# A gated HGRN2 and pooling block: the pool products spread over two gate steps, operand sums one per step, RMS roots computed on GpSimd

## The chip, the cores and the metric

The kernel runs on one core of a Trainium2 chip. The metric is the device time of one execution in microseconds (us); the number that counts is the median over several runs. The engines are named as in the profile: PE is TensorE (PEld its weight loads), DVE is VectorE, ACT is ScalarE, POOL is GpSimd, and SP is SyncE, which in this kernel computes nothing and issues most of the DMAs, in its own order.

## The reference

One decoder block over 1024 tokens of width 1024, all in float32:

```
proj = x @ w_in -> [q | f | i | og | pool_v | gate_a | gate_b]        # 7 x 1024 columns
f = lb + (1 - lb) * sigmoid(f_pre);  k = 1 - f
S_t = diag(f_t) S_{t-1} + k_t v_t^T;  o_t = S_t^T q_t                  # 8 heads of 128, chunks of 16
o = o * rsqrt(mean(o^2) + 1e-6) * hgrn_norm_g * sigmoid(og)            # per head
a = o @ w_a
b = (causal_mean_w(pool_v) - pool_v) @ w_pool[g] * pool_scale          # 4 groups of 256, windows 2, 4, 8, 16
mix = (sigmoid(gate_a) * a + sigmoid(gate_b) * b) @ w_out
x = LN(2^0.25 * x + mix);  x = LN(2^0.25 * x + relu(x @ w_up)^2 @ w_down)
```

## The kernel before

Every large product is done in float32 precision by three products of a high and a low part: an operand is copied on ACT into its high part (line 125) and the rest is taken on DVE into its low part (line 126), so each operand costs one ACT copy and one DVE subtraction. On top of that, a product of two by two blocks is done in seven block products instead of eight, with sums of blocks as operands. The function `pair` writes out these seven steps for one pair of 128 output columns: each step is an operand (`t0`, `b_21`, `t2`, `t3`, `t1`, `t4`, `b_22`) and a product of twelve matmuls of 512 columns (`p1` to `p3`, all through `prod`, lines 206 to 214). The sums of weight blocks are made on DVE in place, in the raw blocks: `make_t3` makes one, and `make_t2` makes two at once (lines 287 to 291). The results of the seven products are put together by copies out of PSUM on ACT (line 274) and sums on DVE (line 278); the `takes` then apply the sigmoid and store the result to a scratch tensor in DRAM.

The middle of the kernel is the recurrence over eight heads and two halves of the tokens. It is a generator, `recurrence`, that hands out small pieces of work. `run` calls it once after every product of twelve matmuls ("a turn"), so the recurrence's small matmuls stand between the large ones. A half takes 8.5 turns (`PER_HALF`). In its first turn come the outputs of the half before (`outputs`), the transposed keys and the scores; in the turn `TURN_BACK` = 4 the outputs are transposed (`turn_outputs`, line 990), multiplied by gain and gate (line 992) and sent off (`put_output`, lines 629 to 637), and the states of the half are made. The other turns prepare the next half, chiefly on DVE, with some small operations on POOL (lines 863 to 882). `outputs` squares the four chunks on ACT with a running sum (line 980), takes the root on ACT (line 981), the reciprocal on DVE (line 982), and scales on ACT (line 984). Sigmoid and root are functions of different ACT tables, so both come with an ACT_TABLE_LOAD.

`ORDER` (line 33) gives the columns that are done beside the recurrence: the inputs of the heads, the pool values (`pooled`), the output gates, and the gates 0 to 6. The order on PE is written out by hand in this part (`manual_schedule`, line 1035); the other engines and SP are ordered by a scheduler that works by a timeline of its own, and the order is then fixed. After the recurrence, lines 1043 to 1048 do `pool_products(0)` to `pool_products(3)` and then `gates(7)`. One `pool_products(g)` loads w_pool[g] and four tiles of pooled values, splits them into high and low parts, and makes four products of six matmuls each into PSUM tiles "pj" (lines 732 to 752). Each is multiplied on DVE by the scale and by a gate that is loaded back (line 751), and stored. The tiles for the loads ("raw", a ring of six) and for the parts of pooled values ("w", a ring of ten) are those of the weight blocks; q, f, v and og of the recurrence hold the gates and results. After that come the product with w_a, in pairs, then w_out with the first norm, then w_up and w_down.

All tiles are rings of a few buffers: a new tile of a ring waits until an older one has been read for the last time, by engines or by DMAs.

Of the kernel before, what the change touches and what calls it, by code (L numbers as in the profile page):

```python
# [11 lines left out]
U32 = mybir.dt.uint32  # L12
AF = mybir.ActivationFunctionType
ALU = mybir.AluOpType
# [16 lines left out]
TURN_BACK = 4  # L31
# [4 lines left out]
    ("gates", 2), ("inputs", 7), ("pooled", 3), ("gates", 3), ("gates", 4), ("gates", 5), ("gates", 6),  # L36
)
PRIO_WHOLE = 6000
# [12 lines left out]
def tile_hybrid_block(  # L51
# [191 lines left out]

    def w_part(src):
        return split(src, w_tile)
# [20 lines left out]
    def pair(raw, rooms, takes, pz_tag="pj", twin=False, pc_tag="pj", turned=False):  # L266
# [18 lines left out]
        def make_t2():  # L285
            if turned:
                V.tensor_sub(b12, b11, b12)
                minus_sum(b11, b22, b12)
            else:
                V.tensor_sub(b12, b12, b11)  # L290
                V.tensor_sub(b11, b22, b12)

# [10 lines left out]

        def t4():
# [8 lines left out]
        def t1():  # L313
            return w_part(b12)
# [106 lines left out]
    with tc.tile_pool(name="xr", bufs=8, side="right", reuse_waits="tile") as xr:  # L421
# [34 lines left out]
        def load_x(u, w):  # L456
            rows_of = x2[u * HALF : (u + 1) * HALF, w].rearrange("(t p) c -> p t c", p=P)
            nc.sync.dma_start(out=x_rows[u][:, :, w], in_=rows_of)
# [30 lines left out]
        load_x(1, slice(HALF, D))  # L489
# [152 lines left out]
    with tc.tile_pool(name="tmp", bufs=1, side="right", reuse_waits="tile") as tmp:  # L642
# [25 lines left out]
        def head_inputs(h, behind=()):  # L668
# [13 lines left out]
            def take_q(u):  # L682
# [5 lines left out]

            run(pair(
                loaded_blocks(w_in, h * P, D + h * P), (c_soon, c_late, room_f),  # L690
# [21 lines left out]
        def gates(j):  # L712
            spare = j == KT - 1
            rooms = [lambda tag=tag: tt(tag) for tag in ("q", "f", "og")] if spare else (c_soon, c_late, c_late)

            def take(dst, src=None, more=None):
                def put(t):
                    s = (tt("v") if spare else c_late()) if src else t
                    more_of = loaded(more, lambda: tt("v")) if more is not None else None
                    A.activation(s, t, AF.Sigmoid)  # L720
                    if more_of is not None:
                        V.tensor_mul(s, s, more_of)
                    nc.sync.dma_start(out=dst if more is None else more, in_=s)
                return put

            more = pbd[j] if spare else (None, None)
            run(pair(
                loaded_blocks(w_in, 5 * D + j * P, 6 * D + j * P), rooms,
                (take(gad[j][0]), take(gbd[j][0], True, more[0]), take(gad[j][1]), take(gbd[j][1], False, more[1])),
            ))  # L730

        def pool_products(g):

            rooms = iter(("v", "q", "f", "og"))
# [300 lines left out]
        with tc.manual_schedule(engines={mybir.EngineType.PE}):  # L1035
# [7 lines left out]
            for _ in turns:  # L1043
                pass
# [441 lines left out]
```

## Time and profile before

| | us |
|---|---|
| median of 3 runs | 1473.27 (1473.22 to 1474.59) |
| the profiled execution | 1472.62 |
| its span in the trace | 1470.8 |
| PE busy in it | 1438.0 |
| DVE busy | 1100.2 |
| ACT busy | 760.8 |
| POOL busy | 107.4 |

The span runs from the first to the last instruction of the program; 1.8 us of the execution's time lie around it. A busy PE is not a PE at full rate: a matmul's end is modelled, so short waits and a lowered clock are seen better in the number of matmuls that fit into a stretch. In the stretches without a wait and with nothing but matmuls of 512 columns, 134 of them fit into 30 us.

The stages by time from the start of the span: the values (up to about 97 us), the recurrence with the columns beside it (to about 606 us), the pool products (about 619 to 650 us), the last gate and w_a, w_out and the first norm (to about 850 us), w_up, and w_down to the end.

### The profile page before, as it was taken

What the parts mean: (1) busy time and instruction counts of PE and PEld (TensorE: products, weight loads), DVE (VectorE), ACT (ScalarE), POOL (GpSimd) and SP (SyncE); (2) the same over time, 40 slices, a digit from 0 to 9 for tenths busy, and PEclk for the clock granted to TensorE, in tenths of its full rate; (3) what the DMA queues carried; (4) which work ended last, traced back from release to release, by engine and by line L of the source; (5) the groups of instructions that cost most, each with busy time, mean ns of one, the idle gap of its engine ahead of it and who ended that gap; (6) DMA issues with size and microseconds to landing.
All of it is one profiled execution on the core that took longest, in us unless ns stands there. A gap on an engine that the chain in (4) does not pass through costs nothing.

```text
span 1470.8 us, 20899 instructions
## 1 busy us (share of the span) xinstructions
PE 1438.0 (98%) x7377; PEld 1189.8 (81%) x7377; DVE 1100.2 (75%) x1807; ACT 760.8 (52%) x1383; POOL 107.4 (7%) x288
## 2 busy tenths in 40 slices
PE   8999999999999999979999999999999999999997
PEld 7788888788878888858788878888888888888886
DVE  4967876896897796467985598566666787777977
ACT  5545566665755655545542366555556543333435
POOL 0002111211211210000002100000000100000000
PEclk9999999999999999989999999999999999999999
DMA  7142245345435536797663134444447874435422
GB/s 258 58 136 87 76 127 165 79 137 152 107 93 145 136 87 174 247 337 256 223 230 114 58 100 174 137 154 156 144 151 264 275 263 150 163 131 170 129 72 115
DMA packets 187738, 229.21 MB, mean 156 GB/s; under 512 B 12240, under 2 KB 110576, under 8 KB 187632
## 3 DMA queue, kind: packets, MB, share of 16 engines
q1 hardware_dynamic: 181664, 213.96, 43.9%
q0 software_dynamic: 5184, 11.54, 4.0%
q10 hardware_dynamic: 784, 2.38, 0.5%
q8 instruction: 58, 0.95, 0.3%
q14 instruction: 48, 0.39, 0.1%
HBM read 150.22 MB, written 77.59 MB: 155 GB/s over the span
## 4 chain that ended last, share of the span: by engine, by line
PE 88%; DVE 5%; DMA 4%; issue 1%; ACT 1%; SPq 0%; POOL 0%; DVEq 0%; ACTq 0%
PE ps_pj L211 15%; PE ps_pj L214 15%; PE ps_pj L213 15%; PE ps_pj L1369 4%; PE ps_pj L1367 4%; PE ps_pj L1368 4%; PE ps_pj L112 2%; PE ps_pj L113 2%; PE ps_pj L114 2%; PE ps_tr L1369 1%; PE ps_tr L1367 1%; PE ps_tr L1368 1%; PE ps_sc L211 1%; PE ps_sc L213 1%; PE ps_sc L214 1%
## 5 line engine op out<-in xcount | busy, mean ns | idle before, releaser
L211 PE MATMUL ps_pj<-act,w 128*128 128x512 f32 x1068 | 420.5, 394 | 8.3 <-ACT c L274 2.9
L214 PE MATMUL ps_pj<-act,w 128*128 128x512 f32 x1068 | 416.0, 391 | 2.3 <-DVE w L126 2.3
L213 PE MATMUL ps_pj<-act,w 128*128 128x512 f32 x1068 | 415.3, 390 | 0.0
L125 ACT CAST w<-raw 128x512 fp32r<-128x512 f32 x326 | 202.3, 622 | 289.8 <-PE ps_pj L213 200.9
L126 DVE TENSOR_TENSOR w<-raw,w 128x512 fp32r<-128x512 f32 x326 | 222.8, 686 | 107.2 <-ACT w L125 101.0
L211 PEld LDWEIGHTS ps_pj<-act,w 128*128 128x128 f32 x1068 | 200.9, 188 | 53.6 <-ACT c L274 4.5
L214 PEld LDWEIGHTS ps_pj<-act,w 128*128 128x128 f32 x1068 | 200.8, 188 | 46.4 <-DVE w L126 3.9
L213 PEld LDWEIGHTS ps_pj<-act,w 128*128 128x128 f32 x1068 | 201.0, 188 | 40.5
L1329 ACT CAST act<-act 128x1024 fp32r<-128x1024 f32 x66 | 67.1, 1050 | 109.0 <-issue 35.0
L278 DVE TENSOR_TENSOR c<-c,ps_pj 128x512 f32<-128x512 f32 x95 | 64.7, 682 | 43.5 <-PE ps_pj L214 41.5
L1368 PE MATMUL ps_pj<-act,act 128*128 128x512 f32 x240 | 93.0, 389 | 0.0
L1369 PE MATMUL ps_pj<-act,act 128*128 128x512 f32 x240 | 93.0, 389 | 0.0
L1330 DVE TENSOR_TENSOR act<-act,act 128x1024 fp32r<-128x1024 f32 x66 | 79.4, 1219 | 17.6 <-ACT act L1329 16.5
L1367 PE MATMUL ps_pj<-act,act 128*128 128x512 f32 x240 | 92.5, 389 | 0.0
L274 ACT COPY c<-ps_pj 128x512 f32<-128x512 f32 x96 | 55.9, 582 | 2.5 <-DMA v<-c 1.3
L1368 PEld LDWEIGHTS ps_pj<-act,act 128*128 128x128 f32 x240 | 45.0, 188 | 9.4
L1369 PEld LDWEIGHTS ps_pj<-act,act 128*128 128x128 f32 x240 | 45.0, 188 | 9.4
L1367 PEld LDWEIGHTS ps_pj<-act,act 128*128 128x128 f32 x240 | 45.0, 188 | 9.3
L283 DVE TENSOR_TENSOR raw<-raw,raw 128x512 f32<-128x512 f32 x43 | 29.6, 689 | 28.2 <-DMA raw<-in_w_in_dram 27.1
L1238 ACT ACTIVATE c<-c 128x512 f32<-128x512 f32 x61 | 38.5, 632 | 1.7
L1237 ACT ACTIVATE c<-c 128x512 f32<-128x512 f32 x46 | 29.1, 632 | 16.6 <-DVE c L278 16.4
L1323 DVE TENSOR_TENSOR act<-act,ps_pj 128x512 f32<-128x512 f32 x45 | 30.1, 681 | 6.0 <-PE ps_pj L1369 5.7
(413 smaller groups left out, 2664.2 us busy)
## 6 DMA issues: line engine op xcount, KB each, us to landing
h<-c SPq DMA_DIRECT2D x106, 256.0 KB, 2.7
raw<-in_w_in_dram SPq DMA_DIRECT2D x100, 256.0 KB, 3.2
act<-h SPq DMA_DIRECT2D x78, 256.0 KB, 3.0
draw<-in_w_down_dram SPq DMA_DIRECT2D x16, 1024.0 KB, 7.7
raw<-in_w_up_dram SPq DMA_DIRECT2D x56, 256.0 KB, 2.8
hf<-h SPq DMA_DIRECT2D x34, 256.0 KB, 3.0
s<-og POOLq DMA_DIRECT2D x28, 256.0 KB, 6.1
v<-v SPq DMA_DIRECT2D x16, 256.0 KB, 3.5
```

What stands on the lines that cost most here:

```text
L125: A.copy(hi, src)
L126: V.tensor_sub(lo, src, f(hi))
L211: PE.matmul(ps, wh[:, k], th, start=first and k == 0, stop=False, skip_group_check=True)
L213: PE.matmul(ps, wh[:, k], tl, start=False, stop=False, skip_group_check=True)
L214: PE.matmul(ps, wl[:, k], th, start=False, stop=k == CH - 1, skip_group_check=True)
L274: A.copy(t, ps)
L278: V.tensor_add(t, t, ps)
L1329: A.copy(hi, src)
L1330: V.tensor_sub(lo, src, f(hi))
L1367: PE.matmul(ps, hh[:, w], wh, start=fresh and n == 0, stop=False, skip_group_check=True)
L1368: PE.matmul(ps, hh[:, w], wl, start=False, stop=False, skip_group_check=True)
L1369: PE.matmul(ps, hl[:, w], wh, start=False, stop=n == M - 1, skip_group_check=True)
```

## The change

Four things are changed.

1. `pool_products` becomes one generator over all groups, and `gates(6)` leaves `ORDER`. `gates(6)` and `gates(7)` now run after `ORDER`, and after each of their seven products `beside` first takes a turn of the recurrence, where one is left, and then as many pool products as `POOL_AFTER` says: 1, 1, 1, 1, 1, 1, 2 and 2, 2, 2, 2, 0, 0, 0. The tiles are other ones: loads go into tA, st and tH (two buffers each) and tC, the parts of w_pool into tD, tE, tF and og, the PSUM tile is "tr" (a ring of two), the loaded gates are in "f" (a ring of four). The loads run two steps ahead. The last group's second half stays in the tile "v", and `gates(7)` multiplies by it.
2. `make_t2` makes one sum, and the other is made in `t1`.
3. The root is taken on POOL: `inverse_root` makes a first guess from the bits of the number and three Newton steps, 14 instructions on 128x4 elements. The scaling becomes `scale_outputs`, in turn 2, behind the latest copy of a high part on ACT; `TURN_BACK` becomes 5.
4. The weight blocks of the first head are issued behind the last load of x.

```diff
+TURN_BACK = 5
+TURN_SCALE = 2
+ROOT_GUESS = float(0x5F3759DF)
+ROOT_STEPS = 3
+POOL_AFTER = {6: (1, 1, 1, 1, 1, 1, 2), 7: (2, 2, 2, 2, 0, 0, 0)}
...
     def w_part(src):
-        return split(src, w_tile)
+        hi, lo = w_tile(), w_tile()
+        last_hi[0] = A.copy(hi, src).ins
+        V.tensor_sub(lo, src, f(hi))
+        return hi, lo
...
-        def make_t2():
-            if turned:
-                V.tensor_sub(b12, b11, b12)
-                minus_sum(b11, b22, b12)
-            else:
-                V.tensor_sub(b12, b12, b11)
-                V.tensor_sub(b11, b22, b12)
+        def make_t2():
+            if turned:
+                minus_sum(b11, c["t"], b11)
+            else:
+                V.tensor_add(b11, c["t"], b11)
...
         def t1():
+            if turned:
+                minus_sum(b12, b22, b11)
+            else:
+                V.tensor_sub(b12, b22, b11)
             return w_part(b12)
...
+            with tc.issue_after(last_x.ins) if not h else nullcontext():
+                blocks = loaded_blocks(w_in, h * P, D + h * P)
...
+        def pool_products():
...
+            pod_tile, w_tiles = ring("tA", "tA", "st", "st", "tH", "tH"), ring("tD", "tE", "tF", "og")
...
+            w_parts = {}
+            todo = [(g, u) for g in range(CH) for u in range(2)]
+            soon = [load(*todo[0]), load(*todo[1])]
+            pl = parts(*todo[0], *soon.pop(0))
+            yield
+            for n, (g, u) in enumerate(todo):
+                if n + 2 < len(todo):
+                    soon.append(load(*todo[n + 2]))
+                wh, wl = w_parts[g]
+                for i in (0, 1) if g < CH - 1 else (1, 0):
...
+                    t = tt("v") if final else loaded(gbd[j][u], lambda: tt("f"))
+                    ps = ps_tile("tr", 2)
                     mm3(ps, [(wh[:, c, w], wl[:, c, w], *pl[c]) for c in range(2)])
-                    if j == KT - 1:
+                    if final:
+                        held[u] = t
                         A.activation(t, ps, AF.Copy, scale=pscale[:, j : j + 1])
                     else:
                         V.scalar_tensor_tensor(t, ps, pscale[:, j : j + 1], t, ALU.mult, ALU.mult)
-                    nc.sync.dma_start(out=pbd[j][u], in_=t)
+                        nc.sync.dma_start(out=pbd[j][u], in_=t)
+                    if i == (1 if g < CH - 1 else 0) and soon:
+                        pl = parts(*todo[n + 1], *soon.pop(0))
+                    yield
+
+        def beside(stream, counts):
+
+            for n in counts:
+                next(turns, None)
+                for _ in range(n):
+                    next(stream, None)
+                yield
...
+        def inverse_root(total):
+
+            x, y, z = (small(tag, [P, CH]) for tag in ("rx", "ry", "rz"))
+            G.tensor_scalar(x, total, 1.0 / P, eps_rms, ALU.mult, ALU.add)
+            G.tensor_scalar(y.bitcast(I32), x.bitcast(I32), -0.5, ROOT_GUESS, ALU.mult, ALU.add)
+            for _ in range(ROOT_STEPS):
+                G.tensor_mul(z, y, y)
+                G.tensor_mul(z, z, x)
+                G.tensor_scalar(z, z, -0.5, 1.5, ALU.mult, ALU.add)
+                G.tensor_mul(y, y, z)
+            return y
...
-                A.activation(ss, ss, AF.Sqrt, bias=eps_rms, scale=1.0 / P)
-                V.reciprocal(ss, ss)
-                for c in range(CH):
-                    A.activation(on[:, chunk(c)], o[:, chunk(c)], AF.Copy, scale=ss[:, c : c + 1])
+                self.o, self.root = o, inverse_root(ss)
+
+            def scale_outputs(self):
+
+                with tc.issue_after(last_hi[0]):
+                    for c in range(CH):
+                        w = chunk(c)
+                        A.activation(self.on[:, w], self.o[:, w], AF.Copy, scale=self.root[:, c : c + 1])
...
+            stream = pool_products()
+            next(stream)
+            for j, counts in POOL_AFTER.items():
+                turning[0] = beside(stream, counts)
+                gates(j)
             for _ in turns:
                 pass
-            for what, j in (
-                ("pool_products", 0), ("pool_products", 1), ("pool_products", 2), ("pool_products", 3), ("gates", 7),
-            ):
-                dict(gates=gates, pool_products=pool_products)[what](j)
+            turning[0] = iter(())
```

More of the change, by code (lines that the diff above doesn't have):

```diff
@@ L12 @@
 U32 = mybir.dt.uint32
+I32 = mybir.dt.int32
 AF = mybir.ActivationFunctionType
@@ L712, in gates, with take @@
         def gates(j):
[L713 to L716 removed]
+            final = j == KT - 1
+            room = (lambda: tt("q")) if final else c_late
+            def take(dst, src=None, u=None):
                 def put(t):
[L718 to L719 removed]
+                    s = (tt("og") if final else c_late()) if src else t
@@ L727, in gates @@
             run(pair(
[L728 to L741 removed]
+                loaded_blocks(w_in, 5 * D + j * P, 6 * D + j * P), (room if final else c_soon, room, room),
@@ L1018, in recurrence @@
                 for turn in range(1, round(at) - round(at - PER_HALF)):
+                    if turn == TURN_SCALE and old:
+                        old.scale_outputs()
                     if turn == TURN_BACK:
```

47 lines of the change are left out of this document (28 added, 19 removed).

## The prediction

> **What bounds the kernel now.** I read the page's busy shares first, then the busy time by stretches of 30 us, then what PE waited for.
>
> ```profile
> span 1470.8 us, 20899 instructions
> PE 1438.0 (98%) x7377; PEld 1189.8 (81%) x7377; DVE 1100.2 (75%) x1807; ACT 760.8 (52%) x1383; POOL 107.4 (7%) x288
> ...
> 570.00:600.00 30.00, 30.00 (x151) 25.28 (x151) 16.20 (x28) 18.49 (x42) 0.86 (x1) 1.00 0.59 174
> 600.00:630.00 30.00, 30.00 (x135) 24.81 (x135) 15.63 (x23) 14.55 (x25) 2.63 (x3) 1.00 0.92 293
> 630.00:660.00 30.00, 22.80 (x80) 16.26 (x78) 19.85 (x31) 13.10 (x23) 0.00 (x0) 0.89 0.93 338
> 660.00:690.00 30.00, 29.67 (x124) 24.40 (x125) 23.21 (x37) 15.79 (x29) 0.00 (x0) 0.94 0.68 214
> 930.00:960.00 30.00, 30.00 (x134) 24.86 (x133) 20.22 (x31) 17.07 (x30) 0.00 (x0) 1.00 0.49 167
> ```
>
> PE is busy for 98% of the span, so the kernel is bound by PE, and a change can only gain where PE waits or runs at a lowered clock, and lose where it makes new waits. The count of matmuls says where: 930 to 960 us is PE at its rate (134 in 30 us, 0.224 us each). 600 to 630 holds 135. 630 to 660 holds 80 and 660 to 690 holds 124: 54 and 10 matmuls are missing, 64 x 0.224 = 14.3 us. This is the stage of the pool products and the start of gates(7), and the change takes it apart. (570 to 600 holds more only because small matmuls of the recurrence are among them.)
>
> ```profile
> 633.55 0.54 PE L112 MATMUL ps_pj<-w,q 128*128 128x512 f32 x1 [2.24 <-ACT q L125]
> 658.58 0.50 PE L211 MATMUL ps_pj<-act,w 128*128 128x512 f32 x1 [1.54 <-ACT w L125]
> ...
> 645.15 0.63 PE L112 MATMUL ps_pj<-w,q 128*128 128x512 f32 x1
> ...
> 625.00:630.00 5.00, 5.00 (x23) 4.13 (x22) 3.35 (x5) 1.65 (x3) 0.00 (x0) 1.00 1.06 406
> 640.00:645.00 5.00, 3.05 (x12) 2.19 (x11) 3.97 (x7) 2.51 (x5) 0.00 (x0) 0.91 1.07 394
> ...
> ACT w L125 <- DMA raw<-po: 10.5, 7, 3.3
> ...
> raw<-po SPq DMA_DIRECT2D x16, 256.0 KB, 5.1
> ```
>
> Why PE waits there: the operand copies on ACT wait 10.5 us in seven waits for the pooled values. The DMA rows carry 406 GB/s at a share of 1.06, and so does 640 to 645 with its 394: the DMA engines are full. The timeline of PE shows a second price: behind a wait of some two us the matmuls take 0.63 instead of 0.39 us for a while, and the clock column falls to 0.91. All of this is in the 14.3 us.
>
> A quick sum says that the stage cannot be otherwise. Its 16 pooled tiles, 4 w_pool blocks, 14 loaded gates and 14 stores are 48 transfers of 256 KB, 12.6 MB. Its 96 matmuls last 21.5 us. That asks for 585 GB/s, and the rows give about 405.
>
> **The pool products among two gate steps.** Two gate pairs are 168 matmuls, so with the 96 they are 264 x 0.224 = 59.1 us of PE. To the 12.6 MB come 8 weight blocks and 8 stores (4.2 MB): 16.8 MB in 59.1 us are 284 GB/s, 70% of what the rows above carry. The DMAs fit, with room for the first loads of w_a and its other operand. The other engines fit too:
>
> ```profile
> L125 ACT CAST w<-raw 128x512 fp32r<-128x512 f32 x326 | 202.3, 622 | 289.8 <-PE ps_pj L213 200.9 <-PE ps_hg L213 17.4 <-PE ps_sc L213 17.3
> L126 DVE TENSOR_TENSOR w<-raw,w 128x512 fp32r<-128x512 f32 x326 | 222.8, 686 | 107.2 <-ACT w L125 101.0 <-PE ps_pj L499 4.8 <-PE ps_hg L499 0.4
> L751 DVE SCALAR_TENSOR_TENSOR f<-ps_pj,prm,f 128x512 f32<-128x512 f32 x4 | 3.0, 746 | 0.5 <-PE ps_pj L114 0.5
> ```
>
> A gate pair has on DVE 7 subtractions, 4 sums of blocks and 3 sums of results, 14 x 0.686 = 9.6 us. The pool products have 20 subtractions and 14 multiplications, 20 x 0.686 + 14 x 0.746 = 24.2 us. With two more multiplications that is 44.8 of 59.1 us, 76%. ACT has less. So the old stall of 14.3 us goes, and what stands in its place are waits of single instructions.
>
> The one that I can point to hangs on the tile og. The low part of the second w_pool block goes into og, which the last half of the recurrence has just filled, and which three accumulating DMAs of POOL still read.
>
> ```profile
> 606.18 0.60 PE L990 MATMUL ps_tr<-ident,tH 128*128 128x128 f32 x4
> 607.05 0.74 DVE L992 SCALAR_TENSOR_TENSOR og<-ps_tr,e,og 128x512 f32<-128x512 f32 x1
> 608.09 2.63 POOL L637 DMA_DIRECT2D s<-og  x3 [24.06 <-DVE og L992]
> ...
> s<-og POOLq DMA_DIRECT2D x3, 256.0 KB, 9.2
> s<-og POOLq DMA_DIRECT2D x3, 256.0 KB, 5.5
> ```
>
> The last transposition ends at 606.8, the multiplication at 607.8, and POOL issues from 608.1. The two DMA rows are the median from issue to landing, of the middle one: 9.2 us here, with the DMAs full, and 5.5 in a lighter window (380 to 385). The third lands about 2 us behind the middle one. So og is free some 7.5 to 12 us behind the multiplication. In the built order of the changed kernel, 38 matmuls (8.5 us) stand between that transposition and the first matmul that reads the part in og. The part is ready 1.0 + 7.5 to 12 + 0.7 us behind the transposition, 9.2 to 13.7, so PE waits 0.7 to 5.2 us. Over 2 us the slow matmuls come on top: some eight in the timeline, at 0.63 instead of 0.39 us, about 1.8. I take 3.0, towards the lighter end, since 284 GB/s is below the full rate. Behind this wait stand on DVE, in order, a sum of the last gate's blocks, the multiplication that empties a "tr" tile, a sum of results and the low part of the next step. PE wants that low part 22 matmuls (4.9 us) later, and four operations are 2.8 us: they catch up.
>
> The rest of the stage: the ring of parts ("w", ten) now serves the pooled values as well. At three steps of gates(6) a weight part is written into a buffer that PE left only 8 matmuls (1.8 us) before the product, and copy and subtraction alone are 0.62 + 0.69. Loads of "f" stand on SP behind the landing of the store that empties the same buffer; a store and a load at the 5.1 us of the row above are 10.2, while four buffers at two products a step go round in 4 x 2.7 = 10.9 us. Neither can be read from the trace of before. I bound them by 0 and 5 us and take 2.0. Stage: -14.3 + 3.0 + 2.0 = -9.3 us, between -14 and -2.5.
>
> **Roots on POOL.** In the recurrence PE waits four times for a copy or a sum out of PSUM:
>
> ```profile
> 265.18 0.50 PE L211 MATMUL ps_pj<-act,w 128*128 128x512 f32 x1 [1.31 <-ACT c L274]
> 290.82 0.50 PE L211 MATMUL ps_pj<-act,w 128*128 128x512 f32 x1 [1.54 <-ACT c L274]
> 433.40 0.50 PE L211 MATMUL ps_pj<-act,w 128*128 128x512 f32 x1 [1.15 <-ACT f L274]
> 437.63 0.50 PE L211 MATMUL ps_pj<-act,w 128*128 128x512 f32 x1 [1.21 <-DVE f L278]
> ...
> 255.44 1.28 ACT L981 ACT_TABLE_LOAD   x1
> 256.73 0.30 ACT L981 ACTIVATE ss<-ss,eps_rms 128x4 f32<-128x4 f32 x1
> 262.21 1.28 ACT L685 ACT_TABLE_LOAD   x1
> 264.55 0.58 ACT L274 COPY c<-ps_pj 128x512 f32<-128x512 f32 x1
> 289.41 0.89 ACT L984 ACTIVATE tH<-ps_hg,ss 128x128 f32<-128x128 f32 x3 [0.41 <-DVE ss L982]
> 290.18 0.60 ACT L274 COPY c<-ps_pj 128x512 f32<-128x512 f32 x1
> ...
> L981 ACT ACT_TABLE_LOAD x16 | 20.5, 1283 | 0.3
> L981 ACT ACTIVATE ss<-ss,eps_rms 128x4 f32<-128x4 f32 x16 | 4.8, 298 | 0.2
> L982 DVE RECIPROCAL ss<-ss 128x4 f32<-128x4 f32 x16 | 2.6, 161 | 3.2 <-ACT ss L981 3.2
> ```
>
> That is 1.31 + 1.54 + 1.15 + 1.21 = 5.2 us. In the first case the copy of 264.55 stands behind a table load of 1.28 at 262.21, in the second behind scalings that waited for the reciprocal. The root goes from ACT in all 16 halves, with its load (1.28), its 0.30 and the load that brings the sigmoid back: 2.9 us of ACT each. The scaling stays, in another place, and now waits for POOL. The fourth wait is for a sum on DVE, which the change relieves by 0.16 and by one moved sum only. So I take 3.0 of the 5.2, between none and all.
>
> The Trainium skill ("ScalarE: Activation LUTs", section "What ACT_TABLE_LOAD costs") gives 1283 ns for the load, as the rows do, and 1380 ns of drain on top. By that a switch frees 2.66 us, and all four waits would go, 5.2 us. The rows show no drain: the root starts at 256.73, where the load ends.
>
> What POOL does for it is bounded by its rows for the same size:
>
> ```profile
> L877 POOL TENSOR_TENSOR eq<-p,p 128x4 f32<-128x4 f32 x16 | 3.8, 235 | 0.0
> L870 POOL TENSOR_TENSOR p<-p 128x8 f32<-128x8 f32 x16 | 11.8, 738 | 1.3
> ```
>
> 14 instructions at 0.235 us are 3.3, at 0.738 they are 10.3. The forms with a scalar and on the number's bits are not in the trace. The nearest row is the first (128x4), so I take some 4 us with the waits between them. Before, root and reciprocal took from 255.44 to about 260.0. The scaling now stands two turns (5.4 us of PE) later, the transposition one turn later, and POOL's own small work for the next half is not urgent. Nothing on the path; if it is late, it is a rival below. The accumulating DMAs on POOL move behind these 14 only by order; og is read back far later.
>
> **Sums one per step; first head behind x.** The sums are as many as before. At the start of w_up DVE makes them in one burst, and PE waits there:
>
> ```profile
> 867.79 0.50 PE L211 MATMUL ps_hg<-act,w 128*128 128x512 f32 x1 [0.81 <-ACT w L125]
> 869.20 0.50 PE L214 MATMUL ps_hg<-act,w 128*128 128x512 f32 x1 [0.67 <-DVE w L126]
> ...
> L290 DVE TENSOR_TENSOR raw<-raw,raw 128x512 f32<-128x512 f32 x38 | 26.1, 686 | 0.5
> ```
>
> Two or three sums of 0.69 us leave the burst before these two waits (0.81 + 0.67), and return a step later. I take 1.0 of 1.5, between 0 and 1.5. The head's blocks stand behind the last x in the built order of before already, so this edit moves no issue: 0.
>
> **Sum.** 9.3 + 3.0 + 1.0 = 13.3 us. The span becomes 1457.5, the execution (1472.62 - 1470.8 = 1.8 us around it) 1459.3, and the median of the runs was 0.65 above the profiled one: 1460.
>
> **Rivals.** (1) The waits of the new stage are at their upper ends: og 5.2 + 1.8 and 5 us for rings and loads, 12.0 in place of 5.0, and the relief of ACT is half. For it: the landing of 9.2 us was measured in this very stage. Against it: the DMAs were full there, and are not now. 1460 + 7.0 + 1.5 = 1468.5. (2) Slower: SP does not feed the DMAs. Some 57 transfers (14.9 MB) stand on it up to the last loaded gate, several behind a landing. PE gives them 250 matmuls, 56 us; below 266 GB/s it waits, and at 190 GB/s (78 us) for 22 us: 1460 - 5 + 22 = 1477. Below 200 GB/s the gain is gone. Against it: this queue carried 406. (3) POOL is late: at 10.3 us and more in 15 halves the scaling holds ACT some 2 to 3 us, with the operand copies and the copies of line 274 behind it, and 15 x 1.5 us beyond the lead make 1483. The Trainium skill ("GPSIMD Engine Reference", sections "4.1 Engine selection" and "8. Key points") sends elementwise work to VectorE, GpSimd being about half as fast and sharing its SBUF interfaces with it; the 0.738 row is in that sense, the 0.235 row is not. (4) All waits go: -14 - 5.2 - 1.5 in place of -13.3, 1452.
>
> **Chances.** Forecast 0.60, rival 1 0.18, rival 2 0.08, rival 3 0.04, rival 4 0.10. The range 1452 to 1470 holds the forecast with its bounds, rival 1 and the near part of rival 4. Runs of this kernel differ by 0.1%, so 0.2% (2.9 us) is about what a measurement tells from no change. Faster than 1470.3: 0.86; within: 0.05; slower: 0.09.
>
> **What would show it.** Right: 134 matmuls in every 30 us from 600 on but for a few; no stretch of DMAs at 1.06 with PE waiting; one wait of PE on a low part written to og, 0.7 to 5 us; two table loads in all before the first norm; POOL's last root instruction ahead of ACT's scaling. Wrong: waits of PE on "tr" products with DMA releasers, ACT waiting on POOL in the halves, or a recurrence that still has four waits of over a us.

## The result, and the profile after

The forecast was 1460 us, faster. The changed kernel takes 1510.3 us (median of four, 1506.7 to 1515.9) against 1473.2 before: 1.0251 of the time, 95% interval 1.0224 to 1.0278. It is slower by 37 us. The profiled execution has a span of 1510.6 against 1470.8, 39.8 us more.

The page of the changed kernel, span, busy shares and the two groups that say most; then those two groups' counterparts of the kernel before, from its groups by line:

```profile
span 1510.6 us, 21024 instructions
PE 1448.0 (96%) x7377; PEld 1194.3 (79%) x7377; DVE 1100.4 (73%) x1791; ACT 713.8 (47%) x1335; POOL 183.3 (12%) x512
...
L216 PE MATMUL ps_pj<-act,w 128*128 128x512 f32 x1068 | 425.8, 400 | 43.0 <-ACT c L284 34.7
...
L1051 ACT ACTIVATE tH<-ps_hg,ry 128x128 f32<-128x128 f32 x64 | 18.3, 368 | 61.5 <-POOL ek L942 35.4
```

```profile
L211 PE MATMUL ps_pj<-act,w 128*128 128x512 f32 x1068 | 420.5, 394 | 8.3 <-ACT c L274 2.9 <-ACT w L125 1.5 <-ACT room L274 1.4
L984 ACT ACTIVATE tH<-ps_hg,ss 128x128 f32<-128x128 f32 x64 | 18.5, 368 | 2.6 <-DVE ss L982 2.4
```

The last column is the idle time of the engine ahead of the group and what ended it. PE's idle time ahead of these products rises from 8.3 to 43.0 us, and 34.7 of it ends with ACT's copy out of PSUM (line 284, 274 before). ACT's idle time ahead of the 64 scalings rises from 2.6 to 61.5 us, and what ends it is POOL, which makes the root. (The page names POOL's latest instruction by its semaphore, ek or eq; the timeline below shows the root's last multiplication there.) ACT itself works 47 us less than before: the table loads did go, all but two ahead of the first norm.

The stretches of 30 us, columns as in the prediction:

```profile
270.00:300.00 30.00, 26.93 (x177) 22.57 (x178) 18.91 (x37) 14.99 (x37) 8.92 (x26) 0.94 0.38 91
330.00:360.00 30.00, 30.00 (x197) 25.11 (x196) 22.42 (x43) 16.62 (x39) 11.68 (x32) 1.00 0.42 99
420.00:450.00 30.00, 23.77 (x98) 19.21 (x97) 24.06 (x54) 10.92 (x25) 8.36 (x25) 0.89 0.28 79
630.00:660.00 30.00, 28.76 (x137) 23.65 (x135) 12.23 (x19) 10.62 (x28) 6.40 (x17) 1.00 0.64 194
660.00:690.00 30.00, 24.09 (x92) 18.54 (x93) 18.28 (x29) 12.20 (x22) 0.00 (x0) 0.89 0.88 287
690.00:720.00 30.00, 28.45 (x124) 23.03 (x123) 24.96 (x40) 17.69 (x32) 0.00 (x0) 1.00 0.83 272
```

PE now stands still in the recurrence, too (270 to 300 and 420 to 450, though a stretch such as 330 to 360 is full), and the stage of the pool products still has its hole, later: 42 matmuls are missing from 660 to 690. Over these 30 us the DMAs' share is 0.88, but while PE stands still, from 658.8 to 664.1, the DMA engines are full, and that at 260 to 266 GB/s in place of the 406 of before:

```profile
658.00:661.00 3.00, 0.76 (x4) 0.28 (x2) 0.00 (x0) 0.00 (x0) 0.00 (x0) 1.00 1.05 260
661.00:664.00 3.00, 0.00 (x0) 0.00 (x0) 0.45 (x1) 1.10 (x3) 0.00 (x0) 0.61 1.09 266
```

To compare kernels whose times shift, I take from the trace, for every two neighbouring matmuls, the distance of their starts, less what it is in undisturbed rows (0.227 us with 512 columns, 0.111 with 128, 0.060 and 0.028 with 64 and 32), and sum it by how much of PE's work is done; every kernel here has the same 7377 matmuls, 1425.8 us by these figures. This is PE's lost time in us, slow matmuls behind a wait included:

| work done (us) | 0-150 start | 150-600 recurrence | 600-700 pool products, last gates, start of w_a | 700-1426 | all |
|---|---|---|---|---|---|
| before | 10.7 | 2.4 | 16.1 | 4.3 | 33.6 |
| changed | 10.4 | 43.7 | 16.3 | 3.2 | 73.6 |
| difference | -0.3 | +41.3 | +0.2 | -1.1 | +40.0 |

The 40.0 are the 39.8 of the spans. All of it is in the recurrence; the pool stage, from which 9.3 us were to come, gave nothing.

One half of the recurrence shows how. Timeline of the changed kernel, start, duration, engine, and in brackets the idle time before and its releaser:

```profile
258.85 0.27 POOL L870 TENSOR_SCALAR rx<-ss,eps_rms 128x4 f32<-128x4 f32 x1 [0.69 <-ACT tH L1043]
261.62 0.54 POOL L926 COPY T<-tA 128x32 f32<-128x32 f32 x1 [2.51 <-DVE tA L909]
262.24 0.47 POOL L871 TENSOR_SCALAR ry<-rx 128x4 int32<-128x4 int32 x1
...
264.10 0.69 POOL L874 TENSOR_TENSOR rz<-rz,rx 128x4 f32<-128x4 f32 x1
264.75 0.38 POOL L935 TENSOR_TENSOR dec<-p 128x4 f32<-128x4 f32 x1
...
266.04 0.19 POOL L875 TENSOR_SCALAR rz<-rz 128x4 f32<-128x4 f32 x1
...
270.46 0.20 POOL L876 TENSOR_TENSOR ry<-ry,rz 128x4 f32<-128x4 f32 x1
...
259.68 0.69 DVE L293 TENSOR_TENSOR raw<-raw,raw 128x512 f32<-128x512 f32 x1 [2.69 <-DMA raw<-in_w_in_dram]
...
270.69 1.14 ACT L1051 ACTIVATE tH<-ps_hg,ry 128x128 f32<-128x128 f32 x4 [3.69 <-POOL c L837]
272.41 0.61 ACT L284 COPY c<-ps_pj 128x512 f32<-128x512 f32 x1
...
273.07 0.80 PE L216 MATMUL ps_pj<-act,w 128*128 128x512 f32 x1 [5.41 <-ACT c L284]
```

The first Newton instruction runs at 258.85. The second is ready then, but POOL's next in order is the copy of T for the half to come. That waits for DVE's scan, and DVE sits behind a sum (line 293) that waits for a weight block from DRAM: 2.5 us. Ten small instructions for the next half (lines 926 to 945) then stand among the steps. The last step ends at 270.66, 11.8 us after the first. ACT has waited 3.69 us for it, the copy out of PSUM behind the scaling is late, and PE stands still for 5.41 us.

### The profile page after: what moved, and what is told of

It reads as the page before. It is cut to its first block, busy times and chain, and to the rows that moved or that the text cites. A ratio compares the mean times of both kernels' runs of the same rounds, so it can differ in the third digit from the quotient of the medians.

```text
span 1510.6 us, 21024 instructions
## 1 busy us (share of the span) xinstructions
PE 1448.0 (96%) x7377; PEld 1194.3 (79%) x7377; DVE 1100.4 (73%) x1791; ACT 713.8 (47%) x1335; POOL 183.3 (12%) x512
## 4 chain that ended last, share of the span: by engine, by line
PE 75%; DVE 8%; POOL 6%; DMA 5%; issue 3%; ACT 3%; SPq 0%; DVEq 0%; ACTq 0%; POOLq 0%
PE ps_pj L216 12%; PE ps_pj L219 12%; PE ps_pj L218 12%; PE ps_pj L1439 3%; PE ps_pj L1440 3%; PE ps_pj L1438 3%; PE ps_pj L119 2%; PE ps_pj L117 2%; PE ps_pj L118 2%; DVE w L254 1%; PE ps_tr L1440 1%; PE ps_tr L1438 1%; PE ps_tr L1439 1%; PE ps_hg L219 1%; PE ps_sc L218 1%
## 5 line engine op out<-in xcount | busy, mean ns | idle before, releaser
L216 PE MATMUL ps_pj<-act,w 128*128 128x512 f32 x1068 | 425.8, 400 | 43.0 <-ACT c L284 34.7
L253 ACT CAST w<-raw 128x512 fp32r<-128x512 f32 x302 | 187.7, 623 | 269.3 <-PE ps_pj L218 192.4
L254 DVE TENSOR_TENSOR w<-raw,w 128x512 fp32r<-128x512 f32 x302 | 206.9, 687 | 129.5 <-ACT w L253 125.0
L216 PEld LDWEIGHTS ps_pj<-act,w 128*128 128x128 f32 x1068 | 203.2, 190 | 94.1 <-ACT c L284 40.4
L219 PEld LDWEIGHTS ps_pj<-act,w 128*128 128x128 f32 x1068 | 202.9, 190 | 46.2 <-DVE w L254 2.8
L218 PEld LDWEIGHTS ps_pj<-act,w 128*128 128x128 f32 x1068 | 203.4, 191 | 41.1
L288 DVE TENSOR_TENSOR c<-c,ps_pj 128x512 f32<-128x512 f32 x95 | 64.9, 683 | 47.3 <-PE ps_pj L219 44.5
L1051 ACT ACTIVATE tH<-ps_hg,ry 128x128 f32<-128x128 f32 x64 | 18.3, 368 | 61.5 <-POOL ek L942 35.4
L1448 POOL DMA_DIRECT2D act<-x x7 | 3.9, 551 | 331.0 <-PE ps_pj L219 330.4
L649 POOL DMA_DIRECT2D s<-og x28 | 25.5, 1172 | 120.7 <-DVE og L1059 120.7
```

The costliest lines, as they stand in the source:

```text
L216: PE.matmul(ps, wh[:, k], th, start=first and k == 0, stop=False, skip_group_check=True)
L218: PE.matmul(ps, wh[:, k], tl, start=False, stop=False, skip_group_check=True)
L219: PE.matmul(ps, wl[:, k], th, start=False, stop=k == CH - 1, skip_group_check=True)
L253: last_hi[0] = A.copy(hi, src).ins
L254: V.tensor_sub(lo, src, f(hi))
L288: V.tensor_add(t, t, ps)
```

## The experiments

Fourteen further kernels, all against the kernel before (median 1473 to 1475 us in these runs). "Root" is the time from the first to the last instruction of the root in POOL's (or DVE's) timeline, mean of the first 14 halves; "ACT" is the idle time ahead of the 64 scalings; the last two columns are PE's lost time as above. The times are medians of several runs; the other columns come from the trace of one run of each kernel.

| kernel | median us | ratio, 95% | root | ACT | recurrence | pool stage |
|---|---|---|---|---|---|---|
| before | 1473.2 | 1 | | 2.6 | 2.4 | 16.1 |
| changed | 1510.3 | 1.0251 (1.0224-1.0278) | 9.3 | 61.5 | 43.7 | 16.3 |
| roots_alone | 1515.4 | 1.0279 (1.0260-1.0298) | 9.3 | 58.3 | 44.5 | 13.6 |
| roots_back | 1476.9 | 1.0022 (1.0006-1.0038) | | 2.2 | 8.0 | 14.8 |
| roots_first | 1490.3 | 1.0099 (1.0069-1.0128) | 6.5 | 25.3 | 22.5 | 16.6 |
| root_one_step | 1508.6 | 1.0232 (1.0214-1.0250) | 6.1 | 40.7 | 43.9 | 14.5 |
| scale_late | 1514.1 | 1.0270 (1.0250-1.0290) | 9.4 | 61.3 | 46.7 | 15.5 |
| roots_dve | 1510.0 | 1.0240 (1.0221-1.0259) | 13.1 | 25.2 | 43.0 | 13.9 |
| prep_dve | 1483.2 | 1.0063 (1.0047-1.0080) | 6.6 | 26.7 | 12.3 | 19.3 |
| scale_behind | 1503.5 | 1.0193 (1.0166-1.0220) | 10.1 | 11.7 | 26.8 | 24.2 |
| first_behind | 1521.1 | 1.0315 (1.0273-1.0358) | 6.5 | 0.0 | 46.0 | 22.8 |
| no_roots | 1467.2 | 0.9946 (0.9929-0.9963) | | 2.7 | 5.4 | 12.0 |
| no_roots_fq | 1467.1 | 0.9949 (0.9932-0.9966) | | 2.2 | 4.1 | 10.9 |
| no_roots_turn5 | 1480.0 | 1.0030 (1.0012-1.0048) | | 2.2 | 9.4 | 17.2 |
| turn5_q | 1476.2 | 1.0012 (0.9998-1.0027) | | 2.2 | 9.3 | 16.2 |
| no_roots_turn3 | 1468.2 | 0.9946 (0.9931-0.9961) | | 1.9 | 3.5 | 13.9 |

**Is it the root?** roots_back undoes it in the changed kernel; roots_alone does it alone in the kernel before, with the new turns of scaling and transposition.

```
roots_back:
         def inverse_root(total):
-            x, y, z = (small(tag, [P, CH]) for tag in ("rx", "ry", "rz"))
...
-            return y
+            A.activation(total, total, AF.Sqrt, bias=eps_rms, scale=1.0 / P)
+            V.reciprocal(total, total)
+            return total
roots_alone (of the kernel before):
-TURN_BACK = 4
+TURN_BACK = 5
+TURN_SCALE = 2
...
+                self.o, self.root = o, inverse_root(ss)
+            def scale_outputs(self):
...
+                    if turn == TURN_SCALE and old:
+                        old.scale_outputs()
```

> The changed kernel with the root of before (Sqrt on ACT, reciprocal on DVE) at the place where the Newton steps stood; all else as changed. Theory A, late roots (the Newton chain on POOL ends after ACT has come to the scaling; ACT, held there, copies PSUM late and PE waits, 41 us from 210 to 600 us): that loss goes, the waits of before behind table loads may return (up to 5 us): 1467 to 1474 us. Rival B, the moved turns (the scaling and the transposition stand at other turns, and hold ACT and PE whoever makes the root): 1500 us or more.

> The kernel before with nothing but the Newton root on POOL, the scaling at turn 2 and the transposition at turn 5; pool products, sums and first head as before. Theory A: the whole loss is here, 1473 + 41, 1509 to 1517 us. Rival C (the recurrence is only slow together with the new order of sums or the pool products in the sixth and seventh gates): 1470 to 1480 us.

1476.9 and 1515.4: the loss comes with the root and goes with it, and needs neither the pool products nor the sums. Rival C falls, and so does B as an account of the 41 us. The moved turn has a price of its own (below), and roots_back is 3 us above its range.

**Which part of the root?**

```
roots_first:
+                    root_last[0] = G.tensor_mul(y, y, z).ins
...
+                with tc.issue_after(root_last[0]) if root_last[0] is not None else nullcontext():
+                    G.tensor_copy(T, blk(fd)[:, :, SUB - 1])
root_one_step:
-ROOT_STEPS = 3
+ROOT_STEPS = 1
scale_late:
-TURN_SCALE = 2
+TURN_SCALE = 4
roots_dve (in inverse_root, and so for all 14):
-            G.tensor_scalar(x, total, 1.0 / P, eps_rms, ALU.mult, ALU.add)
+            V.tensor_scalar(x, total, 1.0 / P, eps_rms, ALU.mult, ALU.add)
prep_dve (in prepare, from T to ek):
-                G.tensor_copy(T, blk(fd)[:, :, SUB - 1])
+                V.tensor_copy(T, blk(fd)[:, :, SUB - 1])
```

> The changed kernel, but POOL's copy of T, and with it the small products behind it for the next half, is issued behind the last Newton step. Theory A1, queue (10 to 12 other POOL instructions and their waits for DVE stand among the 14): the root takes 4.8 us as in the last two halves, ACT's scaling waits under 1 us, 1468 to 1476 us, unless DVE then waits for T. Rival A2, the Newton steps themselves are slow while DVE works: the root still takes 7 us or more, PE still waits in most halves, over 1490 us.

With the 14 in one row the root takes 6.5 us in place of 9.3, and 21 of the 41 us in the recurrence go. More than A1 said stay, and 1490.3 is A2's time, though the root is shorter than A2's 7 us: it is not 4.8 us long while DVE works, ACT still waits 25.3 us at the scalings, and at one place PE waits over 3 us for DVE (whether the later copy of T does that I did not follow).

> The changed kernel with one Newton step in place of three: two steps, 8 of 14 POOL instructions, are left out, the order is otherwise that of the changed kernel. Theory A: the root ends 3.5 to 5 us earlier; the 13 PE waits of 1.0 to 6.4 us shrink by that, some 6 us remain: 1472 to 1482 us. Rival B (moved turns): no change, 1505 us or more.

A miss for theory A: 8 of 14 instructions less, a root 3.2 us shorter, and 1508.6 us all the same. Its ACT timeline shows why that is no proof for B. In the half that was shown above, the scaling now stands four places further forward on ACT, ahead of the copy of tD (line 952), and still waits:

```profile
267.80 0.41 ACT L955 COPY tF<-q 128x256 f32<-128x256 f32 x1
270.83 1.14 ACT L1051 ACTIVATE tH<-ps_hg,ry 128x128 f32<-128x128 f32 x4 [2.63 <-POOL ry L876]
271.85 0.42 ACT L952 COPY tD<-tE 128x256 f32<-128x256 f32 x1
```

I read it so: the planner that orders ACT, DVE and POOL puts the scaling where it expects the root to be done, and expects too early, for 6 instructions as for 14. Its estimate itself is in no trace. The queue in front of the last instruction (T, and DVE behind its weight block) is the same in both.

> The changed kernel with the scaling at turn 4 in place of 2, two turns (5.4 us of PE) later; root, its place on POOL and all else as changed. Theory A (ACT is held at the scaling, because the root ends 7.3 to 12.8 us behind the squares, while ACT comes to it after some 5): at turn 4 most roots are there, of the 41 us 30 or more go, 1474 to 1484 us. Rival B (POOL's added work slows the recurrence in another way, by DVE's waits for T or by a shared path): 1500 us or more.

Nothing was told apart: the built orders of all five engines are the same as in the changed kernel, instruction by instruction. The turn in the code, which the prediction counted as 5.4 us of lead, does not bind ACT's order at all; only PE's order is written by hand. The 1514.1 are the changed kernel run again.

> The changed kernel with the 14 Newton instructions on DVE (VectorE) in place of POOL; scaling at turn 2 as changed. Theory A (the engine's queue and its slow small instructions are the fault): 14 at 0.16 to 0.25 us are 2.2 to 3.5 us of DVE in a half, the root is there in time, 1472 to 1480 us. Rival D (any root of 14 dependent steps comes late, or DVE, which works 73% of the span, falls behind with the low parts): 1485 us or more.

Rival D, in its first half. One instruction costs DVE less than half (rows of lines 873 to 876: 156 to 164 ns, against 299 to 391 on POOL), 14 are 2.3 us, and yet the root takes 9.7 to 17.0 us: the planner spreads the dependent steps among 15 to 37 other DVE instructions. ACT still waits 25.2 us at the scalings, and PE now waits for the scaled rows themselves:

```profile
PE ps_tr L1057 <- ACT tH L1051: 26.4, 7, 5.1
```

> The changed kernel, but the small products and copies for the next half (T to ek, 12 instructions in a half) on DVE; POOL has the 14 Newton instructions alone, the scaling stands where it stood on ACT. Theory A1, queue on POOL: the root takes 5 to 6.5 us, PE waits for the copies behind the scaling shrink to under 1.5 us each, 1472 to 1485 us. Rival A2, 14 dependent steps on POOL are too slow by themselves for this place on ACT: root over 7 us, 1490 us or more. Rival D: DVE, with 12 more instructions in a half, falls behind: waits of PE for DVE's sums and low parts, 1490 us or more.

A1, near its upper end. POOL has the 14 alone, ACT's order is all but that of the changed kernel, and the recurrence loses 12.3 us in place of 43.7; two waits of 1.9 and 2.3 us are longer than A1 allowed. PE's row of prep_dve:

```profile
L216 PE MATMUL ps_pj<-act,w 128*128 128x512 f32 x1068 | 422.6, 397 | 20.6 <-ACT c L284 8.6 <-ACT w L253 8.6 <-ACT room L284 1.2
```

The wait for the copies is 8.6 us in place of 34.7. ACT still stands 26.7 us at the scalings, 1.7 in a half: this much ACT has to spare, the 3.8 of the changed kernel it has not. DVE, with 12 instructions more in a half, does not fall behind: no wait of PE for it in the recurrence is over 1.2 us.

**Can the scaling be put later?** Tied on ACT behind a copy out of PSUM, with the transposition at turn 7:

```
-            A.copy(t, ps)
+            last_copy[0] = A.copy(t, ps).ins
...
-                with tc.issue_after(last_hi[0]):
+                with tc.issue_after(last_hi[0]), tc.issue_after(last_copy[0]):
...
-TURN_SCALE = 2
+TURN_SCALE = 5
+TURN_OUT = 7
first_behind: the same, and the two edits of roots_first
```

> The changed kernel, its root on POOL in the same order, but the scaling tied on ACT behind the last copy out of PSUM that turn 5 knows (the other attempt, turn 4 without such a tie, left every engine's order as it was), and the transposition at turn 7. Theory A (ACT is held at the scaling by the late root, and the copies behind it are what PE waits for): the copies now come first; the recurrence loses 5 to 15 us in place of 44, 1475 to 1487 us. Rival E (not the scaling's place: POOL's longer queue makes the next half's operands late, and DVE, PE wait for these): 1500 us or more.

> As scale_behind, and POOL's copy of T for the next half issued behind the last Newton step, so that the 14 stand in one row. Theory A: root in 6 to 7 us and scaling late enough: 1470 to 1478 us, no wait of ACT for POOL over 0.5 us. Rival E2 (T and what follows on POOL now come 6 us later, DVE waits for them): as roots_first, 1486 us or more.

scale_behind's time is rival E's, its trace is not. No wait of PE of 0.7 us or more for ACT's copies is left between 200 and 600 us, so it was the scaling's place that held them, as A has it. But the recurrence still loses 26.8 us, more than A's 15. What hangs on the scaling and on the transposition now comes later, and that is paid elsewhere: 12.6 us at the products of the states (line 1020), which by the profile start behind the scaling, and one wait of 14 us in the pool stage, for the low part that is written into og:

```profile
PE ps_hg L1020 <- ACT tH L1052: 12.6, 6, 2.5
PE ps_tr L120 <- DVE og L132: 14.0, 1, 14.0
```

first_behind has both edits and both prices, and is the slowest of all, 43 us above the range of A. It also shows a limit of theory A: ACT never waits at the scalings there (0.0 us), and the recurrence loses 46.0 us all the same, 16.7 of them in waits at the products of the states. A root that is in time is not enough; why the parts add up so badly I did not follow further.

**What the rest of the change is worth.** no_roots is the changed kernel with the recurrence of before; no_roots_fq also lets the loaded gates alternate between the buffers of f and q.

```
no_roots:
-                self.o, self.root = o, inverse_root(ss)
+                A.activation(ss, ss, AF.Sqrt, bias=eps_rms, scale=1.0 / P)
+                V.reciprocal(ss, ss)
+                for c in range(CH):
+                    A.activation(on[:, chunk(c)], o[:, chunk(c)], AF.Copy, scale=ss[:, c : c + 1])
...
-TURN_BACK = 5
+TURN_BACK = 4
no_roots_fq (of no_roots):
+            gate_tile = ring("f", "q", "f", "q")
...
-                    t = tt("v") if final else loaded(gbd[j][u], lambda: tt("f"))
+                    t = tt("v") if final else loaded(gbd[j][u], gate_tile)
no_roots_turn5 (of no_roots):
-TURN_BACK = 4
+TURN_BACK = 5
turn5_q (of no_roots_turn5):
-            pod_tile, w_tiles = ring("tA", "tA", "st", "st", "tH", "tH"), ring("tD", "tE", "tF", "og")
+            pod_tile, w_tiles = ring("tA", "tA", "st", "st", "q", "q"), ring("tD", "tE", "tF", "og")
no_roots_turn3 (of no_roots):
-TURN_BACK = 4
+TURN_BACK = 3
```

> The changed kernel with the recurrence as before (root on ACT and DVE, scaling right behind it, transposition at turn 4); the pool products among the gates, the sums one per step and the first head as changed. By the traces, where the changed kernel lost as much in the pool stage as the kernel before (16.3 against 16.1 us of PE) and 1.7 less at the start of w_up: 1470 to 1473 us. By the prediction (9.3 and 1.0 us): 1463 us.

> As no_roots, and the loaded gates of the pool products alternate between the buffers of f (4) and q (3), so that a load no longer waits on SP for the store just issued. Theory F (these waits hold SP's queue, the DMAs run dry and then get nine transfers at once, the load of pooled values into tH lands 7.7 us behind its issue): 4 to 8 us less than no_roots. Rival G (the load into tH is late because the transposition frees tH late and three accumulating DMAs run beside it; the queue of SP does not matter): within 2 us of no_roots.

no_roots beats both kernels: 0.9946 of the time before, 8 us (5 to 10 by the interval), between the two figures expected. no_roots_fq is the same: giving the loaded gates more buffers, so that their loads wait less on SP for a store, gains nothing that can be measured. That is rival G's time, but no test of its reason: the wait for pooled values in tH, which theory F is about, is gone in no_roots already. In the changed kernel F is untested.

That no_roots gains in the pool stage what the changed kernel does not (12.0 against 16.3, and 14.8 in roots_back) pointed at the transposition's turn, which roots_back shares with the changed kernel.

> As no_roots (recurrence as before, pool products and sums as changed), with the transposition and the states at turn 5 in place of 4, as in the changed kernel; nothing of the root or the scaling is moved. Theory H (the later turn frees tH and og later, the pooled values come late into tH in the pool stage and a few copies in the recurrence are late): most of the 8 to 10 us between no_roots and roots_back, 1473 to 1478 us. Rival I (the 8 to 10 us come from the scaling's new place on ACT behind the root, not from the transposition's turn): 1466 to 1470 us.

> As no_roots_turn5, but two of the six tiles that the pooled values are loaded into are buffers of q in place of tH. Theory H1 (the transposition at turn 5 holds tH, whose next load is issued 10.5 us later than with turn 4 and lands 7 us behind its issue beside three accumulating DMAs; PE waits 6.5 us for the part made of it): that wait goes or falls under 2 us, 1470 to 1474 us. Rival H2 (the DMAs are crowded there anyway, the load is late into whichever tile): still 1476 us or more.

> As no_roots with the transposition and the states at turn 3 in place of 4. Theory H (an earlier turn frees tH and og earlier and the later one costs): the wait for the pooled values is gone already, so between 3 us faster and the same as no_roots, 1463 to 1468 us. Rival J (turn 4 is as early as the scaling on ACT and DVE's operands for the states allow; at turn 3 PE waits for them in the recurrence): 1475 us or more.

Turn 5 in place of 4 costs 12.8 us of the medians (10 of the spans), all that lies between no_roots and roots_back and more: theory H, 2 us above its range. PE's timeline of no_roots_turn5, then PE's and DVE's of turn5_q:

```profile
630.76 0.79 PE L216 MATMUL ps_pj<-act,w 128*128 128x512 f32 x1 [6.38 <-ACT w L253]
```

```profile
630.65 0.80 PE L119 MATMUL ps_tr<-w,og 128*128 128x512 f32 x1 [4.69 <-DVE og L131]
...
629.91 0.69 DVE L131 TENSOR_TENSOR og<-tC,tF 128x512 fp32r<-128x512 f32 x1 [5.15 <-DMA o<-og]
```

The first is the wait that the changed kernel has at 664.09 (below): ACT stands at the part of pooled values that are late in tH, and the weight part behind it is late with it. With q in place of tH that wait is gone, and a wait of 4.69 us for og has come in its place. The trace is H1's: the load into another tile is not late. The time, 1476.2, is H2's: 9 us slower than no_roots, and against no_roots_turn5 the two intervals overlap. og comes free by the same transposition, and DVE's low part waits until the last DMA that reads og (o<-og, on SP) has landed. Turn 3 gains nothing over turn 4 (0.9946 both).

## Why the prediction was wrong

Taken one after the other, the ratios divide the way from 0 to +37 us (of 1473): pool products, sums and first head -8; the transposition at turn 5 +12; the root's new place with the old instructions -1 (within its interval); the 14 Newton instructions on POOL alone, its other work on DVE, +6; that other work back among them +28. The intervals of these ratios reach 2 to 4 us to either side, and another order of the steps could divide the way otherwise.

**Roots on POOL, -3.0, is the step that failed.** "Nothing on the path" was wrong on three counts, of which each has its run.
- The 14 instructions were priced alone: "some 4 us with the waits between them". Alone they took 4.8 us in the last two halves, and 6.6 in prep_dve, beside a busy DVE (last section). But POOL runs in order, and "POOL's own small work for the next half is not urgent" overlooked that it need not be urgent to stand in front. With it the root takes 9.3 us (7.2 to 12.7). +28 us of the 37; roots_first, which only puts that work behind the root, wins some 20 of them.
- The lead of "two turns (5.4 us of PE)" does not exist on ACT: scale_late moves the turn and moves nothing. The lead is what the planner makes it, and here it was short of the root by the 3.8 us that ACT waits in a half.
- "The transposition one turn later" was costed at nothing. It frees tH and og a turn later, in the recurrence (+4.0 us of PE's lost time) and in the pool stage (+5.2): no_roots_turn5 against no_roots. These two figures are rough, from one run of each kernel: with the same pool products, the pool stage of the other kernels at turn 5 (those with the transposition at turn 7 left out) loses 13.9 to 19.3.

The 3.0 us themselves, PE's waits that were to go with the table loads, show in no run: prep_dve, which has these loads no more, has 9.4 us of waits for copies and sums in the recurrence, against 5.2 before.

Rival 3 had the mechanism, ACT held at the scaling with the copies of line 274 behind it, and gave it 0.04 and 1483 us. Its price was too small by half: 15 halves at 1.5 us, where ACT waited 3.8 us in each and PE paid 41. Its bound for 14 instructions, 10.3 us, was passed in three of the first 14 halves, with others among the 14, which by themselves took 3.7 to 6.5 us. The Trainium skill ("GPSIMD Engine Reference", section "4.1 Engine selection") sends elementwise work to VectorE, stating GpSimd to be about twice as slow on two inputs; the mean rows agree (156 to 164 against 299 to 391 ns), though POOL's hold waits for DVE (198 ns without them, last section), and by roots_dve the faster engine changes the time by nothing here.

**The pool products, -9.3:** with the transposition at turn 4 the mechanism holds and its size is near, but a price was left out. In no_roots PE's lost time from 600 to 640 us of its work falls from 14.1 to 6.1; from 640 to 700, at the start of w_a, it rises from 2.0 to 5.8, and so the stage gains 4.1. (no_roots as a whole gains 8 by the medians, but 4.2 between the two traces.) In the changed kernel the gain is 0, and no_roots_turn5, with 17.2, says that this is the turn. "The DMAs fit" set 284 GB/s against 405, and that made the engines look emptier than they are: from 600 to 660 no_roots carries 264 to 289 GB/s at a share of 0.86, the kernel before carried 293 at 0.92 (600 to 630, shown in the prediction), and in the stall of the changed kernel 260 to 266 fill them. Why a byte takes more of the engines' time in one stretch than in another is not shown.

The largest wait of the stage was not among the terms: for pooled values loaded into tH. PE, ACT, POOL, SP and DVE in the timeline of the changed kernel:

```profile
664.09 0.79 PE L216 MATMUL ps_pj<-act,w 128*128 128x512 f32 x1 [5.33 <-ACT w L253]
671.11 0.50 PE L119 MATMUL ps_tr<-w,og 128*128 128x512 f32 x1 [1.53 <-DVE og L131]
...
662.90 0.62 ACT L130 CAST w<-tH 128x512 fp32r<-128x512 f32 x1 [9.50 <-DMA tH<-po]
...
654.30 2.70 POOL L649 DMA_DIRECT2D s<-og  x3 [10.11 <-DVE og L1059]
...
655.16 0.43 SPq L627 DMA_DIRECT2D tH<-po  x1
...
670.37 0.69 DVE L131 TENSOR_TENSOR og<-tC,tF 128x512 fp32r<-128x512 f32 x1
```

The load into tH goes out at 655.16, behind the transposition, lands 7.7 us later beside the three accumulating DMAs and other transfers, and ACT stands 9.5 us at its part; the copy of the next weight part waits behind that on ACT. The two waits cost 5.33 + 1.53 and, behind the first, eight matmuls at 0.63 in place of 0.39 us. With turn 4 (no_roots) neither is there: that load goes out at 610.91, beside the same three DMAs, and lands 3.4 us later. So the three are not the reason by themselves; what else in the queue is was not told apart.

The wait of 1.53 us for og lies in the forecast's range (0.7 to 5.2) by luck. The DMAs that read og had all landed by 666.6, and DVE came to the low part at 670.37 without a wait for them: it was late by PE's own stall of 5.33 us. The forecast's mechanism is seen in turn5_q, with 4.69 us, behind a fourth DMA (o<-og) that the prediction did not count.

**Sums one per step, -1.0:** PE's lost time at the start of w_up (830 to 880 us of its work) falls from 4.2 to 2.5 us. The experiments with the new sums have 2.5 to 3.8 there, roots_alone with the old ones 4.2: a gain of 0.4 to 1.7, as forecast. **First head, 0:** the start is the same within 0.3 us.

Rival 2 (SP does not feed the DMAs) did not come true at its 22 us. SP does stand behind a landing in the changed kernel, with no issue from 648.9 to 652.6 us, and the DMAs carry 128 GB/s from 652 to 655; whether that makes the crowd behind it, no run shows.

## What to carry to other kernels

An engine's queue is in order, so a chain of dependent small steps costs what stands among them and what those wait for, not the sum of its instructions: read the built order of every engine the chain passes through, its other work included, and look up what each neighbour waits for. A place in the code, or a turn, is a lead only where it binds the order of the engine that waits; look for the lead in that engine's order, not in the one written by hand. And a step moved one turn later holds every buffer that it would have freed: count who loads into them next. The price of a small POOL instruction is read from a row with the same neighbour on DVE, not from one of the same size (next section).

## What the hardware showed that was not expected

The same 14 POOL instructions run at different rates beside a busy and a less busy DVE. In prep_dve, groups of POOL by line from 255.5 to 262.5 us and from 609 to 615 us:

```profile
L873 POOL TENSOR_TENSOR rz<-ry 128x4 f32<-128x4 f32 x3 | 1.4, 460 | 0.2
L876 POOL TENSOR_TENSOR ry<-ry,rz 128x4 f32<-128x4 f32 x3 | 1.2, 394 | 0.2
```

```profile
L873 POOL TENSOR_TENSOR rz<-ry 128x4 f32<-128x4 f32 x3 | 0.6, 198 | 0.2
L876 POOL TENSOR_TENSOR ry<-ry,rz 128x4 f32<-128x4 f32 x3 | 0.6, 198 | 0.2
```

The two stretches by windows (PE, PEld, DVE, ACT, POOL busy):

```profile
255.60:262.40 6.80, 6.80 (x36) 5.63 (x34) 6.54 (x18) 2.44 (x5) 5.72 (x15) 1.00 0.13 37
609.70:614.50 4.80, 4.80 (x23) 3.95 (x22) 2.18 (x4) 1.05 (x2) 3.69 (x14) 1.00 0.88 294
```

DVE is busy for 6.54 of 6.80 us in the first and 2.18 of 4.80 in the second; the multiplications take 394 to 460 ns there and 198 here. It is not DVE's load as such, but what DVE does at that moment. The same line of the root twice in the changed kernel, each with DVE's instruction beside it:

```profile
266.04 0.19 POOL L875 TENSOR_SCALAR rz<-rz 128x4 f32<-128x4 f32 x1
268.22 0.51 POOL L875 TENSOR_SCALAR rz<-rz 128x4 f32<-128x4 f32 x1
...
265.66 0.68 DVE L288 TENSOR_TENSOR c<-c,ps_pj 128x512 f32<-128x512 f32 x1
268.00 0.68 DVE L961 TENSOR_TENSOR tC<-tE,ek 128x512 f32<-128x512 f32 x1
```

Beside a sum that reads one operand from PSUM POOL takes 0.19 us; beside a product of two tiles in SBUF it takes 0.51, and ends 0.05 us behind DVE's instruction. So it is in the whole trace of the changed kernel: POOL's instructions on 128x4 take 484 ns in the mean beside a TENSOR_TENSOR of two SBUF tiles (158 of them), 195 beside one that reads PSUM (31), and 200 with DVE idle (80). The Trainium skill states that GpSimd shares its SBUF interfaces with VectorE, and that they contend where VectorE's instruction has two SBUF inputs ("GPSIMD Engine Reference", section "8. Key points"); these rows agree.

This is also what parts the two rows that bounded the root in the prediction. Of the 16 instructions of the 235 ns row, 14 stand beside a RECIPROCAL or a COPY_PREDICATED and take 202 to 209 ns; of the 738 ns row, 12 stand beside one product of two SBUF tiles and take 754 to 758. In the changed kernel the instruction of the first row has neighbours of the second kind, and takes 450 ns:

```profile
L940 POOL TENSOR_TENSOR eq<-p,p 128x4 f32<-128x4 f32 x16 | 7.2, 450 | 0.0
```
